# ScalarE's stores issued by GpSimd, the first head's loads put ahead, and the attention outputs split by ScalarE and GpSimd

## The chip, the cores and the metric

The kernel runs on one core of one Trainium2 chip. A core has five engines with an instruction queue each: TensorE (PE, with its weight loads shown apart as PEld), VectorE (DVE), ScalarE (ACT), GpSimd (POOL) and SyncE (SP), and 16 DMA engines that move what any of the queues issues. An engine works through its queue in order: an instruction that waits for a semaphore holds all that stand behind it. The metric is the device time of one execution in microseconds, the median of several.

## The reference

One step of a one-layer decoder over 1024 prompt tokens and 8 x 8 sample tokens: half an FFN, a mixer, and half an FFN again. The mixer joins windowed attention (12 heads of 64) with gated linear attention (4 heads).

```python
h = rmsnorm(x)                        # d_model 1024
x = x + 0.5 * (silu(h @ w1) * (h @ w3)) @ w2            # FFN 1, d_ff 2816
qa, ka, va, qb, kb, vb, rb, glr = split(rmsnorm(x) @ w_in)
qa, ka = rmsnorm(qa) * q_gain, rmsnorm(ka) * k_gain     # per head
oa = merge(dilated_attention(qa, ka, va) + bias)        # windows 128, 512, 2048; prompt
                                      # sample tokens: over 2048 cached keys and the new ones
ob, state = gla(qb, kb, vb, gk)       # chunks of 16
ob = rmsnorm(ob) * silu(rb)
x = x + concat(oa, ob) @ w_out
x = x + 0.5 * (silu(h2 @ w1) * (h2 @ w3)) @ w2          # FFN 2
# returned: x, the keys and values of the windows, the GLA states
```

## The kernel before

Activations lie transposed: 128 channels on the partitions, the 1088 tokens along the free axis. The large products are done in three matmuls each: every operand is split into a high part, rounded to fp32r, and a low part, the rest (`split`, L127: a copy to the high part by one engine, a subtraction for the low part by another; `eh` and `el` choose them, ScalarE and GpSimd where nothing is said). `hH` and `hL` hold the split input of a product, `hl` the split weights, `raw` the weights as loaded.

The program is written as generators, and a scheduler sets each engine's order from its own estimate of times; no order is written out by hand. In time it runs: FFN 1, a norm, the projections, the prompt attention, the output projection, FFN 2.

**The projections** (`inputs`, L309). A unit is 128 columns of the weights in three chunks of tokens, 24 matmuls `psg` each: first those of the linear attention, then values `v`, then queries and keys `q` in turn, then gates `r`. VectorE takes each chunk out of PSUM into a tile `z` (four of them). A chunk of values is turned by TensorE into `psv`, copied to `v` by ScalarE (L431, L433) and stored three ways, to `out_vp`, `vnew` and `out_wv_s` (`turn_values`, L434 to L439). A chunk of queries or keys is normed and stored by GpSimd (`finish_qk`, L473). A chunk of gates is stored to `gsc` by ScalarE (`finish_gate`). Beside this runs the attention of the sample tokens (`sample`, L778): for each of six head pairs SyncE loads a bias `sbias` (L799), keys `kt` (L774) and values `vt` (L794, 512 KB each, six tiles), and ScalarE stores new keys `sko` to `out_wk` and results `soT` to `osc` in two stores (L907). The queries and keys of the sample tokens reach that part through GpSimd's copies `sqk`, `sqs` and into `kt`, which stand behind the stores of L473 in GpSimd's queue.

**The prompt attention** (`attention`, L914) goes over 12 heads. `load(h)` brings queries and keys in as `f` (L929, from `qsc` and `out_kT`, where L473 put them), the bias (L937) and, for each second head, values `va`; VectorE splits them with a cast and a subtraction into `q` and `kk` (L932 to L935); from the second head on GpSimd does the subtraction. Per head: scores `psS` (L962), VectorE adds the bias into `e` (L969), ScalarE's exponential (L982), transposes `psT` and copies `pt`, the weighted sum `psO` (L1022), and VectorE's product into `o` (L1032). When 512 tokens of a head pair are there, `o` is split into `hH` and `hL` (L1035, 12 times). Beside it run the states of the linear attention (`linear_states`, L581; loads `g` from `gsc` and `asc`).

**The output projection** (`out_proj`, `pso`) takes `hH` and `hL`; its weights are split by ScalarE and GpSimd.

A DMA reports its end on a semaphore. In the built program SyncE's and ScalarE's DMAs take turns on eight semaphores (DMAHW0 to 7), GpSimd's on eight others (DMASW0 to 7). A DMA that takes one again first waits, on its own engine's queue, for the end of the transfer that used it last.

Of the kernel before, what the change touches and what calls it, by code (L numbers as in the profile page):

```python
# [9 lines left out]
F32 = mybir.dt.float32  # L10
# [6 lines left out]
P = 128  # L17
# [103 lines left out]
class _Kernel:  # L121
# [299 lines left out]
    def turn_values(self, pool, ps, z, m, ci):  # L421
        nc, a = self.nc, self.a
        cols = slice(128 * m, 128 * m + 128)
        t0, nt = 3 * ci, 3 if ci < 2 else 2
        p = ps.tile([P, 512], F32, tag="b", name="psv")
        for t in range(nt):
            nc.tensor.transpose(p[:, 128 * t : 128 * t + 128], z[:, 128 * t : 128 * t + 128], self.ident)
        if ci == 2:
            nc.tensor.transpose(p[:64, 256:384], z[:, 256:320], self.ident)
        v = pool.tile([P, 3, 128], F32, tag="t1", name="v", bufs=4)  # L430
        nc.scalar.copy(v[:, :nt].rearrange("p t c -> p (t c)"), p[:, : 128 * nt])  # L431
        if ci == 2:
            nc.scalar.copy(v[:64, 2], p[:64, 256:384])  # L433
            nc.scalar.dma_start(out=self.vnew[:, cols], in_=v[:64, 2])  # L434
            nc.scalar.dma_start(
                out=a["wv_s"].rearrange("b (r c) -> b r c", c=768)[:, 2040:2048, cols], in_=v[:64, 2]
            )
            self.vdone = m + 1
        nc.scalar.dma_start(  # L439
            out=a["vp"][128 * t0 : 128 * (t0 + nt), cols].rearrange("(t p) c -> p t c", p=P), in_=v[:, :nt]  # L440
        )

    def finish_gate(self, z, m, ci):
        nc = self.nc
        nc.scalar.activation(z, z, AF.Silu)
        nc.scalar.dma_start(
            out=self.gsc[3 * ci : 3 * ci + 3, :, 5 + m].rearrange("t p r -> p t r"),
            in_=z.rearrange("p (t r) -> p t r", t=3),
        )
# [131 lines left out]
    def linear_states(self, pool, ps):  # L581

        nc, a = self.nc, self.a
        st = pool.tile([P, 9, 64], F32, tag="st", name="st", bufs=2)
        nc.gpsimd.memset(st[:, 0], 0.0)
        ms = pool.tile([P, 3, 36], F32, tag="gms", name="gms")
        qm = []
        for z in range(2):
            t = pool.tile([P, 4, 8, 32], F32, tag="qm", name="qm", bufs=2)
# [46 lines left out]
        for T in range(9):  # L636
            g, kdT, bl = nxt
# [9 lines left out]
            p = ps.tile([P, 512], F32, tag="T", name="psR", bufs=4)  # L647
# [130 lines left out]
    def sample(self, pool, ps, loadk):  # L778
# [18 lines left out]
        for i in range(6):  # L797
# [19 lines left out]
            nc.scalar.dma_start(  # L817
# [88 lines left out]
            for e in range(2):  # L906
                nc.scalar.dma_start(  # L907
                    out=self.osc[i, 64 * e : 64 * e + 64].rearrange("p (b t) -> p b t", t=8), in_=t[:, :, e]
                )
# [4 lines left out]
    def attention(self, inputs, pool, ps):  # L914
        nc = self.nc
        heads = {}

        def load(h):
# [19 lines left out]
            if e == 0:  # L938
                v = pool.tile([P, 8, 128], F32, tag="v", name="va", bufs=2)
                nc.sync.dma_start(  # L940
                    out=v, in_=self.a["vp"][:, 128 * i : 128 * i + 128].rearrange("(t p) c -> p t c", p=P)
                )
            else:
                v = heads[h - 1][3]
            heads[h] = (q, kh, kl, v, b)

        def scores(h, g):

            q, kh, kl, v, b = heads[h]
# [59 lines left out]
        def weigh(h, g, es, pts):  # L1009
            i, e = h // 2, h % 2  # L1010
            r = slice(64 * e, 64 * e + 64)
            v = heads[h][3]
# [20 lines left out]
            if g % 2 and e == 1:  # L1033
                z = slice(512 * (g // 2), 512 * (g // 2) + 512)
                self.split(outs.pop((i, g // 2)), self.hH[:, i, z], self.hL[:, i, z], eh="dve", el="dve")  # L1035
# [5 lines left out]
        load(0)  # L1041
# [105 lines left out]
    def run(self):  # L1147
        nc, tc, a = self.nc, self.tc, self.a
        self.gready, self.done, self.vdone = False, 0, 0
        with ExitStack() as top:  # L1150
# [122 lines left out]
            with ExitStack() as hs:  # L1273
                hpool(hs)
                with ExitStack() as bs:
# [4 lines left out]
                    _interleave(tc, [(self.attention(ip, ap, ps0), 0), (states, 0)])  # L1280
# [166 lines left out]
```

## Time and profile before

| | |
|---|---|
| median of 3 runs | 2401.41 us (2400.91 to 2404.52) |
| the profiled execution | 2401.93 us, span 2400.1 us |
| busy, share of the span | PE 98%, PEld 92%, DVE 48%, ACT 27%, POOL 17% |
| the stages, us from the span's start | FFN 1 48 to 788; norm to 825; projections to 1244; prompt attention to 1519; output projection to 1640; FFN 2 to 2400 |
| PE busy, projections with the sample attention (941 to 1255) | 294.01 of 314 us |
| PE busy, prompt attention (1270 to 1519) | 232.12 of 249 us |
| PE busy, FFN 1 and FFN 2 | 739.70 of 739.70 and 756.76 of 760 us |

The shares are averages over stages with different limits. "Granted clock" is the share of TensorE's full speed that the throttle allowed in a stretch. In the rows a releaser behind an arrow (`<-`) is what ended an engine's idle time; an engine's name with a q (ACTq, SPq) is its queue issuing a DMA.

### The profile page before, as it was taken

To read this page: it belongs to the slowest core of one execution; us is meant where nothing else is said; L and a number is where in the kernel's file an instruction comes from. 1 tells how busy PE (TensorE), PEld (TensorE's weight loads), DVE (VectorE), ACT (ScalarE), POOL (GpSimd) and SP (SyncE) were. 2 spreads that over 40 slices of the span, in tenths; PEclk is the share of its full clock that TensorE was granted. 3 is DMA by queue.
4 is the path that set the end of the run, shared out by engine and by line. 5 is a ranking of instruction groups with operands and counts; after the bars stand their busy time and mean duration, and the time that the engine had idled before them with its cause. 6 is when DMAs were issued, how large, how long until landed. Compare 5 with 4: busy or idle time off the path is not lost.

```text
span 2400.1 us, 38321 instructions
## 1 busy us (share of the span) xinstructions
PE 2341.4 (98%) x16073; PEld 2215.0 (92%) x16073; DVE 1155.9 (48%) x2377; ACT 656.9 (27%) x1347; POOL 408.3 (17%) x303
## 2 busy tenths in 40 slices
PE   7999999999999998999989999999999999999999
PEld 6999999999999987978767767999999999999999
DVE  8452434344342753555538887435444342434333
ACT  5111020101101522545436666334111101020110
POOL 5011020101100400011103231333101101020100
PEclk9999999999999999999999999999999999999999
DMA  7346542524250334599865442414244243111002
GB/s 258 110 162 192 191 152 97 210 97 153 86 196 23 134 131 108 179 342 341 310 184 130 111 115 74 156 36 158 88 163 153 92 154 143 45 53 45 28 17 85
DMA packets 135261, 330.25 MB, mean 138 GB/s; under 512 B 25920, under 2 KB 105264, under 8 KB 127408
## 3 DMA queue, kind: packets, MB, share of 16 engines
q1 hardware_dynamic: 116464, 316.39, 38.7%
q10 hardware_dynamic: 16512, 5.11, 0.9%
q0 software_dynamic: 2112, 6.29, 0.7%
q8 instruction: 126, 2.06, 0.3%
q14 instruction: 47, 0.39, 0.0%
HBM read 300.55 MB, written 134.56 MB: 181 GB/s over the span
## 4 chain that ended last, share of the span: by engine, by line
PE 89%; DVE 5%; DMA 3%; ACT 2%; issue 1%; SPq 1%; POOL 0%; ACTq 0%; DVEq 0%; POOLq 0%
PE ps L306 42%; PE ps L257 21%; PE psg L306 12%; PE pso L306 4%; PE psO L1022 2%; PE psS L962 2%; PE psW L880 1%; PE psT L1001 1%; DMA vt<-in_vin 1%; PE psA L831 1%; DVE hL L155 1%; DVE e L969 1%; PE pss L459 1%; DMA f<-out_kT 0%; DVE rstd L170 0%
## 5 line engine op out<-in xcount | busy, mean ns | idle before, releaser
L306 PE MATMUL ps<-hH,hl 128*128 128x362 f32 (+1 forms) x4224 | 1044.1, 328 | 8.1 <-ACT hl L130 6.8
L306 PEld LDWEIGHTS ps<-hH,hl 128*128 128x128 f32 x4224 | 746.6, 188 | 12.4 <-ACT hl L130 6.7
L306 PE MATMUL ps<-hL,hl 128*128 128x362 f32 (+1 forms) x2112 | 691.5, 328 | 2.9 <-DVE hL L155 2.9
L257 PE MATMUL ps<-g,hl 128*128 128x362 f32 (+1 forms) x3168 | 529.2, 328 | 0.0
L257 PEld LDWEIGHTS ps<-g,hl 128*128 128x128 f32 x3168 | 527.0, 188 | 0.0
L134 POOL TENSOR_TENSOR hl<-raw,hl 128x1024 fp32r<-128x1024 f32 (+1 forms) x98 | 242.8, 2498 | 1223.3 <-ACT hl L130 1223.3
L306 PEld LDWEIGHTS ps<-hL,hl 128*128 128x128 f32 x2112 | 397.5, 188 | 4.9 <-DVE hL L155 3.9
L306 PE MATMUL psg<-hH,hl 128*128 128x384 f32 (+3 forms) x1200 | 312.4, 334 | 0.0
L262 DVE SCALAR_TENSOR_TENSOR xT<-ps,xT 128x362 f32<-128x362 f32 (+1 forms) x384 | 204.6, 534 | 200.3 <-PE ps L257 191.4
L217 ACT ACTIVATE t<-t 128x364 f32<-128x364 f32 x132 | 66.9, 508 | 786.0 <-DVE t L216 785.8
L218 DVE TENSOR_TENSOR t<-ps,rstd 128x364 f32<-128x364 f32 x132 | 70.6, 535 | 417.9 <-PE ps L306 417.9
L306 PEld LDWEIGHTS psg<-hH,hl 128*128 128x128 f32 (+1 forms) x1200 | 211.3, 186 | 12.8 <-issue 8.9
L306 PE MATMUL psg<-hL,hl 128*128 128x384 f32 (+3 forms) x600 | 200.1, 334 | 0.1
L130 ACT CAST hl<-raw 128x1024 fp32r<-128x1024 f32 (+2 forms) x148 | 124.1, 886 | 187.3 <-PE ps L306 109.9
L130 ACT CAST g<-t 128x364 fp32r<-128x364 f32 x132 | 65.2, 494 | 346.8 <-DVE t L219 346.8
L134 DVE TENSOR_TENSOR g<-t,g 128x364 fp32r<-128x364 f32 x132 | 107.1, 813 | 92.8 <-ACT g L130 92.5
L216 DVE TENSOR_TENSOR t<-ps,rstd 128x364 f32<-128x364 f32 x132 | 70.5, 535 | 156.6 <-PE ps L306 155.3
L306 PEld LDWEIGHTS psg<-hL,hl 128*128 128x128 f32 (+1 forms) x600 | 111.7, 186 | 9.3 <-issue 6.7
L134 DVE TENSOR_TENSOR hl<-raw,hl 128x384 fp32r<-128x384 f32 (+3 forms) x178 | 102.9, 587 | 23.9 <-ACT hl L130 19.9
L962 PE MATMUL psS<-kk,q 128*128 128x512 f32 (+2 forms) x288 | 92.2, 411 | 19.6 <-DVE s L969 11.9
L306 PE MATMUL pso<-hH,hl 128*128 128x362 f32 (+1 forms) x384 | 93.6, 325 | 0.2 <-DVE o L1032 0.2
L982 ACT ACTIVATE e<-e,s 128x128 f32<-128x128 f32 (+3 forms) x96 | 74.9, 780 | 43.7 <-DVE s L969 43.1
(205 smaller groups left out, 2007.2 us busy)
## 6 DMA issues: line engine op xcount, KB each, us to landing
out_wk<-in_ck SPq DMA_DIRECT2D x16, 3060.0 KB
out_wv_s<-in_cv SPq DMA_DIRECT2D x16, 3060.0 KB
kt<-in_kin SPq DMA_DIRECT2D x24, 1280.0 KB
vt<-in_vin SPq DMA_DIRECT2D x60, 512.0 KB
raw<-in_w13b SPq DMA_DIRECT2D x22, 1024.0 KB
raw<-in_w13a SPq DMA_DIRECT2D x21, 1024.0 KB
raw<-in_w2a SPq DMA_DIRECT2D x48, 192.0 KB
raw<-in_w2b SPq DMA_DIRECT2D x48, 192.0 KB
```

Of the source, the lines that this page charges most:

```text
L130: nc.scalar.copy(hi, x)
L134: e.tensor_tensor(out=lo, in0=x, in1=hi.bitcast(F32), op=ALU.subtract)
L155: nc.vector.scalar_tensor_tensor(out=self.hL[:, k, s], in0=x, scalar=g, in1=self.hH[:, k, s].bitcast(F32), op0=ALU.mult, op1=ALU.subtract)
L216: nc.vector.tensor_tensor(out=t1[:, :n], in0=p1[:, :n], in1=r, op=ALU.mult)
L217: nc.scalar.activation(t1[:, :n], t1[:, :n], AF.Silu)
L218: nc.vector.tensor_tensor(out=t3[:, :n], in0=p3[:, :n], in1=r, op=ALU.mult)
L257: self.mm(p[:, :n], lhsT=hl[:, wt, j, :], rhs=g[:, gp, :n], start=i == 0, stop=i == 3 * nf - 1)
L262: nc.vector.scalar_tensor_tensor(out=xs, in0=p[:, :n], scalar=0.5, in1=xs, op0=ALU.mult, op1=ALU.add)
L306: self.mm(p[:m, :n], lhsT=hl[:, wt, k, cs], rhs=h[:, k, h0 : h0 + n], start=i == 0, stop=i == 23)
L962: self.mm(p[:, :mm], lhsT=q[:, 128 * n : 128 * n + 128], rhs=kk[:, o : o + mm], start=x == 0, stop=x == 1,)
L982: nc.scalar.activation(e[:, :w], e[:, :w], AF.Exp, scale=-1.0, bias=s[:, j : j + 1], accum_out=s[:, 2:3])
L1022: self.mm(p[64 * n : 64 * n + 64, :128], lhsT=v[:, k, r], rhs=pts[k // 2][k, n], start=k == 0, stop=k == 2 * g + n, tile_position=(0, 64 * n),
```

## The change

Three things are changed. Six `dma_start` calls (54 DMAs in all: 18 to `out_vp`, 6 each to `vnew`, `out_wv_s`, `gsc` and `out_wk`, 12 to `osc`) are issued by GpSimd and no longer by ScalarE. The first head's `load(0)` gets a higher priority in the scheduler, `linear_states` comes first in the interleaving, and the first `va` is loaded there; the `va` tiles move to another pool. The 12 splits of `o` use the default of `split`: the copy by ScalarE, the subtraction by GpSimd.

```diff
@@ turn_values, finish_gate
-            nc.scalar.dma_start(out=self.vnew[:, cols], in_=v[:64, 2])
-            nc.scalar.dma_start(
+            nc.gpsimd.dma_start(out=self.vnew[:, cols], in_=v[:64, 2])
+            nc.gpsimd.dma_start(
                 out=a["wv_s"].rearrange("b (r c) -> b r c", c=768)[:, 2040:2048, cols], in_=v[:64, 2]
             )
             self.vdone = m + 1
-        nc.scalar.dma_start(
+        nc.gpsimd.dma_start(
             out=a["vp"][128 * t0 : 128 * (t0 + nt), cols].rearrange("(t p) c -> p t c", p=P), in_=v[:, :nt]
...
-        nc.scalar.dma_start(
+        nc.gpsimd.dma_start(
             out=self.gsc[3 * ci : 3 * ci + 3, :, 5 + m].rearrange("t p r -> p t r"),
@@ linear_states
         nc.gpsimd.memset(st[:, 0], 0.0)
+        self.load_v(pool, 0)
@@ sample
-            nc.scalar.dma_start(
+            nc.gpsimd.dma_start(
                 out=a["wk"].rearrange("b (r c) -> b r c", c=768)[:, 2040:2048, 128 * i : 128 * i + 128], in_=ko
...
-                nc.scalar.dma_start(
+                nc.gpsimd.dma_start(
                     out=self.osc[i, 64 * e : 64 * e + 64].rearrange("p (b t) -> p b t", t=8), in_=t[:, :, e]
@@ attention
-    def attention(self, inputs, pool, ps):
+    def load_v(self, pool, i):
+        v = pool.tile([P, 8, 128], F32, tag="v", name="va", bufs=2)
+        self.nc.sync.dma_start(
+            out=v, in_=self.a["vp"][:, 128 * i : 128 * i + 128].rearrange("(t p) c -> p t c", p=P)
+        )
+        self.values[i] = v
+
+    def attention(self, inputs, pool, vpool, ps):
...
-            if e == 0:
-                v = pool.tile([P, 8, 128], F32, tag="v", name="va", bufs=2)
...
-            else:
-                v = heads[h - 1][3]
-            heads[h] = (q, kh, kl, v, b)
+            if h % 2 == 0 and h:
+                load_v(i)
+            heads[h] = (q, kh, kl, b)
...
-                self.split(outs.pop((i, g // 2)), self.hH[:, i, z], self.hL[:, i, z], eh="dve", el="dve")
+                self.split(outs.pop((i, g // 2)), self.hH[:, i, z], self.hL[:, i, z])
...
-        load(0)
+        with self.tc.high_priority(offset=300):
+            load(0)
@@ run
-                    _interleave(tc, [(self.attention(ip, ap, ps0), 0), (states, 0)])
+                    _interleave(tc, [(states, 0), (self.attention(ip, ap, gp, ps0), 0)])
```

The scheduler sees the whole program, so the order moves in more places than the diff. Three places follow; numbers behind names are buffer numbers, and "waits" names the semaphores on which a row waits.

ScalarE, in the projections, around the copies of the values (`v_7962` is the last chunk of its unit). Before:

```order
L431 COPY v_7928<-psv_7924 128x384 [waits DMAHW5_49,PE_49]
L439 DMA out_vp<-v_7928 128x3x128 [waits DMAHW1_49,Activation_49]
L431 COPY v_7962<-psv_7958 128x256 [waits DMAHW6_49,PE_49]
L433 COPY v_7962<-psv_7958 64x128
L439 DMA out_vp<-v_7962 128x2x128 [waits DMAHW0_49,Activation_49]
L434 DMA vnew_67<-v_7962 64x128 [waits DMAHW2_49,Activation_49]
L435 DMA out_wv_s<-v_7962 8x8x128 [waits DMAHW4_49]
L431 COPY v_8006<-psv_8002 128x384 [waits PE_49]
L439 DMA out_vp<-v_8006 128x3x128 [waits DMAHW6_49,Activation_49]
```

The same place on ScalarE with the change:

```order
L431 COPY v_7928<-psv_7924 128x384 [waits DMASW5_49,PE_49]
L431 COPY v_7962<-psv_7958 128x256 [waits DMASW6_49,PE_49]
L433 COPY v_7962<-psv_7958 64x128
L431 COPY v_8006<-psv_8002 128x384 [waits DMASW1_49,DMASW0_49,DMASW7_49,PE_49,Activation_49]
L130 CAST hl_8080<-raw_7861 128x512 [waits DMAHW7_49,PE_49]
```

And GpSimd with the change, some way on, where the first stores of the sample results stand among those of L473:

```order
L473 DMA out_kT<-z_8716 128x384 [waits DMASW3_49,DVE_49]
L908 DMA osc_71<-soT_8833 512x1x8 [waits DMASW4_49,Activation_49]
L908 DMA osc_71<-soT_8833 512x1x8 [waits DMASW5_49]
L473 DMA out_kT<-z_8792 128x384 [waits DMASW6_49,DVE_49]
L473 DMA out_kT<-z_8864 128x256 [waits DMASW7_49,DVE_49]
L475 COPY sqk_6871<-z_8864 128x64 [waits Pool_49]
L828 COPY kt_8956<-sqk_6871 128x8x8 [waits DMAHW3_49,PE_49,Pool_49]
```

No store stands between ScalarE's copies any more. On GpSimd the stores of `osc`, which wait for ScalarE's `soT`, now stand between two stores of L473, ahead of the copies for the sample keys.

SyncE, from the last `vt` load on, at the passage from the projections to the prompt attention. Before, and then with the change:

```order
L794 DMA vt_10909<-in_vin 128x1024 [waits PE_49]
L940 DMA va_11135<-out_vp 128x8x128 [waits DMAHW5_49,DVE_49,Pool_49]
L940 DMA va_11349<-out_vp 128x8x128 [waits DMAHW6_49,Activation_49]
L929 DMA f_11121<-qsc_66 64x1024 [waits DMASW2_49,DMAHW0_49,DMASW1_49,DMASW0_49]
L929 DMA f_11121<-qsc_66 64x1024 [waits DMAHW1_49]
L929 DMA f_11127<-out_kT 64x1024 [waits DMASW5_49,DMAHW2_49,DMASW4_49,DMASW3_49]
L929 DMA f_11127<-out_kT 64x1024 [waits DMAHW3_49]
L937 DMA bias_11123<-Z_73 128x1024 [waits DMAHW4_49,PE_49]
L596 DMA g7_11144<-gsc_68 128x640 [waits DMAHW5_49]
```

```order
L795 DMA vt_10909<-in_vin 128x1024 [waits DMAHW7_49,DMAHW0_49,PE_49]
L937 DMA f_11133<-qsc_66 64x1024 [waits DMASW2_49,DMASW3_49,DMASW1_49,DVE_49]
L937 DMA f_11133<-qsc_66 64x1024 [waits DMAHW1_49]
L937 DMA f_11139<-out_kT 64x1024 [waits DMASW6_49,DMAHW2_49,DMASW5_49,DMASW4_49]
L937 DMA f_11139<-out_kT 64x1024 [waits DMAHW3_49]
L945 DMA bias_11135<-Z_73 128x1024 [waits DMAHW4_49,PE_49]
L917 DMA va_11122<-out_vp 128x8x128 [waits DMAHW5_49]
L597 DMA g7_11129<-gsc_68 128x640 [waits DMAHW6_49,Pool_49]
```

The first head's four loads stand right behind the last `vt` and ahead of the values; the DMAHW semaphores on which SyncE waits there no longer alternate with stores of ScalarE.

ScalarE, at the passage from the prompt attention to the output projection. Before, and then with the change:

```order
L1004 COPY pt_14846<-psT_14841 128x512 [waits PE_49,Activation_49]
L1018 COPY rb_14856<-psO_14854 128x128 [waits PE_49]
L130 CAST hl_14891<-raw_14887 128x1024 [waits DMAHW3_49,DMAHW4_49,DMAHW2_49,DMAHW7_49,DMAHW1_49,Pool_49]
L130 CAST hl_14891<-raw_14887 128x1024
L130 CAST hl_14930<-raw_14889 128x1024 [waits DMAHW6_49,DMAHW2_49,Pool_49]
```

```order
L1010 COPY pt_14846<-psT_14841 128x512 [waits PE_49,Activation_49]
L1024 COPY rb_14856<-psO_14854 128x128 [waits PE_49]
L130 CAST hH_11106<-o_14606 128x512 [waits DVE_49]
L130 CAST hl_14891<-raw_14887 128x1024 [waits DMAHW3_49,DMAHW4_49,DMAHW1_49,Pool_49]
L130 CAST hl_14891<-raw_14887 128x1024
```

The copy of the last `o`, which waits for VectorE, now stands ahead of the first weights' copy.

## Rows read from the trace of the kernel before

**Rows 1.** The page: its span, and the chain of work that ended last by engine.

```profile
span 2400.1 us, 38321 instructions
...
PE 89%; DVE 5%; DMA 3%; ACT 2%; issue 1%; SPq 1%; POOL 0%; ACTq 0%; DVEq 0%; POOLq 0%
```

**Rows 2.** Busy time in stretches of the span: from and to, length, then of each engine the busy time with its instructions in brackets, the granted TensorE clock, the DMA engines' busy share and GB/s.

```profile
941.00:1255.00 314.00, 294.01 (x2273) 245.71 (x2272) 150.50 (x311) 135.72 (x286) 31.99 (x84) 0.97 0.79 267
...
1244.00:1276.00 32.00, 19.76 (x164) 14.11 (x164) 22.52 (x59) 14.81 (x38) 10.82 (x9) 0.79 0.71 186
...
1270.00:1400.00 130.00, 121.45 (x1502) 94.69 (x1500) 110.20 (x331) 86.88 (x238) 36.87 (x26) 0.97 0.43 116
```

**Rows 3.** For what TensorE waited in the whole span: total us, times, longest.

```profile
PE psS L962 <- DVE s L969: 11.9, 11, 2.0
PE psv L427 <- ACT v L431: 8.8, 1, 8.8
PE psS L962 <- DVE kk L934: 6.9, 1, 6.9
...
PE psO L1022 <- ACT rb L1018: 4.7, 4, 2.2
```

**Rows 4.** ScalarE and its queue in order of time, around 949: start, us, instruction, and the idle time before it with what ended it.

```profile
937.04 0.26 ACT L433 COPY v<-psv 64x128 f32<-64x128 f32 x1
954.63 0.38 ACTq L439 DMA_DIRECT2D out_vp<-v  x1
...
956.82 0.64 ACTq L435 DMA_DIRECT2D out_wv_s<-v  x1
957.51 0.48 ACT L431 COPY v<-psv 128x384 f32<-128x384 f32 x1 [20.20 <-DMA vt<-in_vin]
```

**Rows 5.** The chain of waits through the same stretch: start, us, what.

```profile
936.74 4.19 PE psg L306 x24
...
946.20 10.60 DMA vt<-in_vin
```

**Rows 6.** Busy time in stretches, columns as in rows 2.

```profile
958.00:962.00 4.00, 3.96 (x14) 3.93 (x15) 1.42 (x3) 1.56 (x4) 0.00 (x0) 0.50 1.01 374
...
1000.00:1200.00 200.00, 196.76 (x1630) 157.50 (x1623) 113.03 (x238) 98.35 (x210) 24.90 (x66) 1.00 0.93 328
1200.00:1244.00 44.00, 43.90 (x329) 37.26 (x327) 9.82 (x21) 12.21 (x25) 1.42 (x5) 1.00 0.49 160
```

**Rows 7.** For what SyncE's queue waited from 960 to 1240: total us, times, longest.

```profile
SPq L794 <- PE psW L880: 73.9, 25, 11.2
```

**Rows 8.** A store on GpSimd's queue in order of time.

```profile
1045.82 0.54 POOL L473 DMA_DIRECT2D out_kT<-z  x1 [10.88 <-DVE z L468]
```

**Rows 9.** A store of the sample results on ScalarE's queue in order of time.

```profile
1044.99 0.55 ACTq L907 DMA_DIRECT2D osc<-soT  x1
```

**Rows 10.** DMA issues from 941 to 1244: how many, KB each, median us from issue to landing.

```profile
qsc<-z POOLq DMA_DIRECT2D x12, 192.0 KB, 6.0
```

**Rows 11.** SyncE's queue in order of time, at the start of the prompt attention.

```profile
1238.26 6.00 SPq L929 DMA_DIRECT2D f<-qsc  x2
1245.28 1.11 SPq L929 DMA_DIRECT2D f<-out_kT  x2
...
1253.65 1.10 SPq L929 DMA_DIRECT2D f<-qsc  x2
```

**Rows 12.** VectorE in order of time, in the same stretch.

```profile
1244.28 0.21 DVE L404 TENSOR_TENSOR zr<-psg,rstd 128x64 f32<-128x64 f32 x1
1247.33 1.03 DVE L932 CAST q<-f 128x1024 fp32r<-128x1024 f32 x1 [2.83 <-DMA f<-qsc]
1248.39 1.22 DVE L933 TENSOR_TENSOR q<-f,q 64x1024 fp32r<-64x1024 f32 x1
1249.98 0.69 DVE L934 CAST kk<-f 128x1024 fp32r<-128x1024 f32 x1 [0.36 <-DMA f<-out_kT]
```

**Rows 13.** The chain of waits in the same stretch.

```profile
1247.54 5.51 DMA g<-asc
...
1255.99 7.79 DMA f<-out_kT
```

**Rows 14.** What writes `hH` from 1270 to 1519, different shapes apart: times, shortest/median/longest ns, first and last start.

```profile
L132 DVE CAST hH<-o x11: 421/428/2131, 1296.2 to 1511.4; 128x512 fp32r<-128x512 f32 x11
L134 DVE TENSOR_TENSOR hL<-o,hH x11: 673/689/2327, 1298.0 to 1512.6; 128x512 fp32r<-128x512 f32 x11
...
L130 ACT CAST hH<-so x1: 512/512/512, 1325.0 to 1325.0; 128x384 fp32r<-128x384 f32 x1
...
L134 POOL TENSOR_TENSOR hL<-gob,hH x9: 456/730/1169, 1342.6 to 1508.2; 128x256 fp32r<-128x256 f32 x8, 128x128 fp32r<-128x128 f32 x1
```

**Rows 15.** The chain of waits from 1270 to 1519.2, shares by line.

```profile
by line: PE psO L1022 17.6%; PE psS L962 17.1%; PE psT L1001 10.8%; issue 6.2%; DVE e L969 5.8%; PE psE L709 3.3%; DVE hL L134 2.9%; PE psD L666 2.8%; ACT e L982 2.5%; DVE o L1032 2.4%; PE psE L704 2.4%; DVE hH L132 2.2%; DVE kk L934 2.2%; 
```

**Rows 16.** All engines in order of time, at the start of the output projection.

```profile
1516.21 3.92 ACT L130 CAST hl<-raw 128x1024 fp32r<-128x1024 f32 x4
...
1516.40 1.97 PE L1022 MATMUL psO<-pt,va 128*64 128x128 f32 x30 [0.89 <-ACT rb L1018]
...
1518.30 0.43 PE L306 MATMUL pso<-hH,hl 128*128 128x364 f32 x1
...
1518.47 0.59 DVE L1032 TENSOR_TENSOR o<-psO,rb 64x128 f32<-64x128 f32 x2 [2.48 <-PE psO L1022]
```

More of the change, by code (lines that the diff above doesn't have):

```diff
@@ L937, in load, with load_v @@
             nc.sync.dma_start(out=b, in_=bass.AP(z.tensor, z.offset + 127, [[GW - 1, P], [1, NP]]))
-            if e == 0:
-                v = pool.tile([P, 8, 128], F32, tag="v", name="va", bufs=2)
-                nc.sync.dma_start(
-                    out=v, in_=self.a["vp"][:, 128 * i : 128 * i + 128].rearrange("(t p) c -> p t c", p=P)
-                )
-            else:
-                v = heads[h - 1][3]
-            heads[h] = (q, kh, kl, v, b)
+            if h % 2 == 0 and h:
+                load_v(i)
+            heads[h] = (q, kh, kl, b)
+        def load_v(i):
+            self.load_v(vpool, i)
         def scores(h, g):
-            q, kh, kl, v, b = heads[h]
+            q, kh, kl, b = heads[h]
             out = []
@@ L1011, in weigh @@
             r = slice(64 * e, 64 * e + 64)
-            v = heads[h][3]
+            v = self.values[i]
             if g % 2 == 0 and e == 0:
@@ L1149, in run @@
         self.gready, self.done, self.vdone = False, 0, 0
+        self.values = {}
         with ExitStack() as top:
```

## The prediction

> **What bounds it now.** I read the page first: TensorE's own work is 89% of the chain that ended last, of 2400.1 us [rows 1]. The FFNs, two thirds of the time, are not touched, so the change can only win back idle time of TensorE, or time at the lower clock, between 941 and 1520 us. The view by stretches shows how much there is: 20 us idle in 941 to 1255, 12 of 32 us at the start of the prompt attention, 8.5 of 130 us further on in it [rows 2]. Then the table of waits, which puts names to it: 8.8 us once for ScalarE's copy `v`, 6.9 us once for the first keys' cast on VectorE, and in the prompt attention 11.9 us in eleven waits for VectorE's `s` and 4.7 us for ScalarE's `rb` [rows 3]. The change has one part for each of the first three.
>
> **A, the stores on GpSimd.** ScalarE ended its copy at 937.30 and its next store could be issued only at 954.63; the following copy, for which TensorE stood from 949 on, began at 957.51 after 20.20 us, 17 of them before that first store [rows 4]. The data of the stores had long been there. The chain reaches the last of these stores through the landing of a `vt` load, 10.60 us [rows 5]: a load of SyncE that shares nothing with the store but the semaphore. In the order of before each store stands between two copies and waits on a DMAHW semaphore; with the change no store is there, and GpSimd's stores wait only on DMASW, for older stores of GpSimd. So the 8.8 us go. After the gap TensorE ran four microseconds at a granted 0.50, which is 1.2 of 2.4 GHz [rows 6]; at full clock the same work takes 2.0. A = 10.8 us. Lower bound 7, if the clock stays low and a wait is left as long as the longest for `s`, 2.0 [rows 3]; upper 11.
>
> Can TensorE keep the lead? From 1000 to 1200 the DMA engines are 0.93 busy and TensorE idles 3.2 of 200 us [rows 6]. But SyncE's queue waited there 73.9 us for TensorE to free `vt` tiles [rows 7]: loads follow TensorE, not the other way, and the share falls to 0.49 at the end of the stretch [rows 6]. The whole stretch moves forward together.
>
> What the stores cost GpSimd: 54 issues at 0.54 us, the time of one of its stores now [rows 8], against 0.55 on ScalarE [rows 9], are 29 us on an engine busy 32 of 314 us [rows 2]. Beside TensorE that is nothing. The stores of `osc` have 512 pieces each, of a kind that GpSimd does not issue before; below, the same 0.54; above, the 6.0 us that its stores take to land [rows 10], if it were held for so long. I take 0.54, since both engines' issue times are alike.
>
> The Trainium skill ("DMA: Bandwidth & Descriptors", section "Issuing engines are not separate DMA queues") says that all queues feed the same 16 DMA engines and that issuing from another engine saves only the issuing time. By that A would be nothing and the sum 2392. The gap in rows 4 is not issuing time but a wait ahead of it, which the page does not speak of.
>
> **B, the first head's loads.** Now SyncE's `f` loads of head 0 stand behind both `va`; their issue takes from 1238.26 to 1246.39, because the semaphores alternate with stores, and head 1's follow at 1253.65 [rows 11]. VectorE, done with the gates at 1244.49, waits 2.83 us for queries and ends the keys' cast at 1250.67 [rows 12]. With the change all four loads stand right behind the last `vt`, so that they can land before the projections end. VectorE's order still puts the casts behind the gates: 1244.5 + 1.03 + 1.22 + 0.69 (the durations in rows 12) gives 1247.5, which is 3.2 us earlier. The path goes on through head 1's loads, in the chain with 5.51 us for `g` and 7.79 us for `f` [rows 13]. These need head 0's first `f` tile, which the subtraction frees at 1249.61 [rows 12]; the 4 us from there to 1253.65 are the semaphores. So 3.2 for the tile and 4 for them: 7 us earlier. I take 7, since the chain runs through head 1; bounds 3 (head 0's gain alone) and 10 (with clock won back, 0.79 there [rows 2]).
>
> **C, the splits.** Eleven casts of 428 ns and eleven subtractions of 689 ns (medians, the longest 2131 and 2327 [rows 14]) leave VectorE in the stretch. On the chain they are 2.2% and 2.9% of 249.2 us [rows 15], 12.7 us. ScalarE gets 12 copies; the nearest, 128x384, took 512 ns [rows 14], so 0.6 each, 7 us in all: it has room (86.88 of 130 busy [rows 2]) but TensorE waits for it too, 4.7 us for `rb` [rows 3]. GpSimd gets 12 subtractions at twice the 730 ns of 128x256 [rows 14], less what an instruction costs anyway: an estimate of 1.3 each, 15 us, with 36.87 of 130 busy [rows 2]. VectorE is only one of several engines that end last here, so I take half of the 12.7: C = 6, from nothing to 12.
>
> The Trainium skill ("SBUF — State Buffer", section "Who interferes with whom") says that a VectorE instruction with two SBUF inputs and a GpSimd instruction that reads SBUF exclude each other for a whole instruction. By that 12 subtractions of 1.3 us would block VectorE up to 15 us, against the 12.3 us of work at median length (eleven times 0.428 + 0.689) that leave it: C would be nothing, and the sum 2387. The trace agrees that some such thing is there: medians of 428 and 689 ns stand beside longest ones of 2131 and 2327 [rows 14].
>
> **E, a loss.** At the passage to the output projection ScalarE now begins the weights' copy at 1516.21, four of them in 3.92 us, and `pso` starts at 1518.30, as the last `psO` ends at 1518.37 [rows 16]. With the change the last `o`'s copy stands ahead of it in ScalarE's order; that `o` is done 0.7 us after the last `psO` (1519.06 [rows 16]). So 0.7 + 0.6 for the copy + 1.0 for the first weights' copy: `pso` starts 2.4 us after `psO`, and some low clock after it, an estimate of 1 from rows 6. E = 3.5, from 2 to 4.5. The first product's low weights come later still on GpSimd, behind the last subtraction; I count that as covered by the matmuls on high weights.
>
> **Sum.** 2400.1 - 10.8 - 7 - 6 + 3.5 = 2379.8 us of span; the profiled execution took 1.8 us more than its span, so 2381.6, and it lay 0.5 above the median: **2381 us**. With all lower bounds (7, 3, 0, -4.5) 2396, with all upper ones (11, 10, 12, -2) 2370.
>
> **Rivals.**
> 1. *A is given back.* The transfers run on the same 16 engines, 0.93 busy from 1000 on, and TensorE waits for `vt` or `kt` instead: 2381 + 10.8 = 2392. For it: that share. Against it: SyncE's waits for TensorE.
> 2. *C is nothing:* ScalarE takes VectorE's place in the waits of `psO` and `psT`, or GpSimd's subtractions stretch VectorE's work: 2387.
> 3. *The loads are early, but it does not help:* casts remain behind the gates in VectorE's order and head 1 comes no earlier: B is 3, 2385.
> 4. *Slower: GpSimd's queue.* In it the stores of `osc` now stand, waiting for `soT`, ahead of stores of normed queries and keys. If `soT` comes late, the four `z` tiles stay occupied, VectorE cannot take the next chunk and TensorE stops. The store behind it waited 10.88 us for its own data, and was issued at 1045.82, 0.8 us after `osc` on ScalarE [rows 8, 9]: today the two are about even. Three free tiles are three chunks of 24 matmuls, 4.19 us each [rows 5], so 12 us of slack. From 12 us on each microsecond counts, six times: with 17 us it is 6 x 5 = 30, 2411. The same end comes if a store holds GpSimd near the 6.0 us of its landing.
>
> **How the numbers follow.** Forecast 0.55; rival 1 0.13; rival 2 0.13; rival 3 0.05; the first two together (2398) 0.05; rival 4 0.09. The range 2370 to 2397 is the sum's two ends; it holds rivals 1 to 3 and most of the forecast, and leaves out some 0.17. A difference of 0.2%, 4.8 us, is about what a measurement of this kernel can tell. Faster by more: the forecast, 0.11 of rival 1, all of rivals 2 and 3: 0.84. The same: 1 and 2 together and what is left of rival 1 and 4, 0.09. Slower: 0.07.
>
> **What would show it.** A: no wait of `psv` for ScalarE over 1 us, and the clock whole from 949 to 962. B: `psS` waits 3 to 4 us, not 6.9, and TensorE's idle time in the 32 us from the end of the projections falls from 12 to about 5. C: `hH<-o` and `hL<-o` on ScalarE and GpSimd, waits of `psS` for `s` shorter. E: a wait of the first `pso` for ScalarE of 2 to 3 us. I am wrong if TensorE idles more than 6 us between 1000 and 1244 (old clock), if GpSimd's new stores take over 1 us each, or if `rb` and `e` take over the waits of `s`.

## The result, and the profile after

The changed kernel takes 2384.25 us (median of 4 runs, 2383.22 to 2385.45), the kernel before 2401.16 (2397.02 to 2404.52) on the same chip: a ratio of 0.9931, with a 95% interval of 0.9913 to 0.9948. It is 0.7% faster, 17 us, where 20 were forecast. The profiled execution has a span of 2383.0 us. Its page, span and chain, as [rows 1]:

```profile
span 2383.0 us, 38378 instructions
...
PE 91%; DVE 4%; DMA 2%; issue 1%; ACT 1%; POOL 0%; SPq 0%; DVEq 0%; ACTq 0%; POOLq 0%
```

The chain has two points more of TensorE, and less of VectorE, DMA and ScalarE. For what TensorE waited, as [rows 3] (line numbers up to 8 higher than before, since the file grew):

```profile
PE psS L968 <- DVE s L975: 6.1, 11, 1.3
...
PE psS L968 <- DVE kk L942: 3.2, 1, 3.2
PE psW L881 <- DMA vt<-in_vin: 2.8, 3, 1.7
PE pso L306 <- ACT hl L130: 2.4, 1, 2.4
...
PE psO L1028 <- ACT rb L1024: 0.4, 1, 0.4
```

The 8.8 us of `psv` are not there at all; the keys' cast costs 3.2 us and not 6.9, the waits for `s` 6.1 and not 11.9, `rb` 0.4 and not 4.7. New are 2.4 us in which the first `pso` waits for ScalarE, and `psW` waits for `vt` loads, 2.8 us.

To see where the time went, I read six moments from both timelines (us from the span's start, in the profiled executions):

| | before | after | earlier by | won in this stretch |
|---|---|---|---|---|
| the 720th `psg`, just behind the gap at 949 | 968.50 | 955.61 | 12.9 | 12.9 |
| end of the last `psg` | 1243.90 | 1236.45 | 7.4 | -5.5 |
| first `psS` | 1250.82 | 1239.68 | 11.1 | 3.7 |
| end of the last `psO` | 1518.36 | 1497.16 | 21.2 | 10.1 |
| first `pso` | 1518.30 | 1499.52 | 18.8 | -2.4 |
| end of the span | 2400.1 | 2383.0 | 17.1 | -1.7 |

Of the first 12.9 us, 2.1 were there by 870, ahead of the change's places: from 858 to 864 the mean granted clock was 0.72 in the execution before and 1.00 in the one after, and among the kernels below it is 0.72 in some (e1, e3 and e7 among them) and 1.00 in others (e2, e5 and e9 among them). No edit touches this place, and I don't count the 2.1 as the change's; but where one kernel was profiled twice (after and e5, e4 and e6) both have 1.00, so whether it is chance or the order of the work stays open. The gap itself gave 10.8: from the 600th `psg`, ahead of it, to the 720th it is 32.04 us before and 21.25 after.

**A.** GpSimd's queue in the stretch of [rows 4], start, us, instruction, idle time and what ended it:

```profile
944.52 0.75 POOL L439 DMA_DIRECT2D out_vp<-v  x1 [3.75 <-ACT v L431]
948.24 0.72 POOL L439 DMA_DIRECT2D out_vp<-v  x1 [2.96 <-ACT v L433]
948.95 0.56 POOL L434 DMA_DIRECT2D vnew<-v  x1
949.51 0.62 POOL L435 DMA_DIRECT2D out_wv_s<-v  x1
```

The three stores that held ScalarE for 17 us are issued as soon as ScalarE's copy is there. And the price of four kinds of store, the first a kind that GpSimd issued before, from 930 to 1240 us (busy us, mean ns, idle before):

```profile
L473 POOL DMA_DIRECT2D qsc<-z x18 | 9.9, 552 | 75.9 <-DVE z L468 75.8
L439 POOL DMA_DIRECT2D out_vp<-v x11 | 8.2, 748 | 30.5 <-ACT v L431 17.5 <-ACT v L433 12.9
L908 POOL DMA_DIRECT2D osc<-soT x12 | 8.2, 694 | 40.2 <-ACT soT L906 40.2
L446 POOL DMA_DIRECT2D gsc<-zr x6 | 4.6, 762 | 17.3 <-ACT zr L445 17.3
```

A store of `osc` with its 512 pieces costs 694 ns to issue, one of `gsc` 762, against 0.54 us that I took. Nothing is near the 6.0 us of the upper bound. But between 1000 and 1236 some of the lead is lost again. Two stretches there (columns as in [rows 2]):

```profile
1000.00:1018.00 18.00, 16.33 (x134) 13.48 (x134) 9.97 (x19) 10.53 (x23) 2.60 (x8) 1.00 0.98 298
1018.00:1022.00 4.00, 4.00 (x35) 2.14 (x38) 0.00 (x0) 0.00 (x0) 0.00 (x0) 0.57 0.98 392
```

In the first TensorE stood 1.67 us, `psW` waiting for a `vt` load; behind it the granted clock fell to half, 0.57 in the mean of these four microseconds. That is not all of the 5.5 us: idle time grew by 1.4 (3.24 to 4.65) and the half clock cost 1.7, so some 2.3 are left, and they are busy time of TensorE at full clock. The same 2158 matmuls behind the 720th `psg` keep it busy 272.0 to 272.7 us in before, e2, e3 and e8, and 274.9 to 275.7 in e1, e4 to e7 and e12, the kernels with all 54 stores moved, with the clock whole in all of them. What makes them longer, the runs don't show.

**B.** SyncE's queue and VectorE at the start of the attention, as [rows 11, 12]:

```profile
1219.25 1.16 SPq L937 DMA_DIRECT2D f<-qsc  x2
1220.57 1.90 SPq L937 DMA_DIRECT2D f<-out_kT  x2
...
1238.93 1.11 SPq L937 DMA_DIRECT2D f<-qsc  x2
```

```profile
1236.83 0.21 DVE L404 TENSOR_TENSOR zr<-psg,rstd 128x64 f32<-128x64 f32 x1
1236.96 0.68 DVE L940 CAST q<-f 128x1024 fp32r<-128x1024 f32 x1
...
1238.93 0.69 DVE L942 CAST kk<-f 128x1024 fp32r<-128x1024 f32 x1
```

The first head's loads are issued 17 us ahead of the last `psg`, so VectorE goes from the gates straight to the casts, and head 1's queries are loaded 2.5 us after the last `psg` (1238.93 against 1236.45), where it was 9.8 us before (1253.65 against 1243.90). In the 32 us from the last `psg` on, TensorE idles 7.0 us, not 12 (the prediction had 5).

**C.** What writes `hH` and `hL` of `o`, as [rows 14], and the whole attention before and after, from the first `psS` to the last `psO` (columns as in [rows 2]):

```profile
L130 ACT CAST hH<-o x12: 603/619/644, 1279.5 to 1497.9; 128x512 fp32r<-128x512 f32 x12
L134 POOL TENSOR_TENSOR hL<-o,hH x12: 1270/1284/1463, 1283.5 to 1498.6; 128x512 fp32r<-128x512 f32 x12
```

```profile
1250.80:1518.40 267.60, 247.64 (x2902) 193.24 (x2902) 212.45 (x646) 177.16 (x475) 69.89 (x49) 0.95 0.40 109
```

```profile
1239.70:1497.20 257.50, 241.58 (x2901) 187.61 (x2901) 199.14 (x624) 180.09 (x483) 84.72 (x62) 0.97 0.41 115
```

The prices were right: 0.62 us on ScalarE, 1.28 on GpSimd. The last two rows tell more. It is the same work, some 2900 matmuls in both; yet TensorE is busy 247.64 us in the one and 241.58 in the other, at a mean granted clock of 0.95 and 0.97. Of the 10.1 us won, 6.1 are busy time, matmuls that ran faster, and 4.0 are idle time (19.96 to 15.92 us).

**E.** The start of the output projection, as [rows 16], and the clock right after it:

```profile
1499.37 2.94 ACT L130 CAST hl<-raw 128x1024 fp32r<-128x1024 f32 x3
1499.52 0.67 PE L306 MATMUL pso<-hH,hl 128*128 128x364 f32 x1 [2.35 <-ACT hl L130]
```

```profile
1499.50:1503.00 3.50, 3.48 (x12) 3.49 (x13) 0.00 (x0) 2.81 (x3) 3.50 (x3) 0.54 0.57 157
```

`pso` waits 2.35 us for the first weights' copy, and runs its first 3.5 us at 0.54.

### The profile page after: what moved, and what is told of

It reads as the page before. It is cut to its first block, busy times and chain, and to the rows that moved or that the text cites. A ratio compares the mean times of both kernels' runs of the same rounds, so it can differ in the third digit from the quotient of the medians.

```text
span 2383.0 us, 38378 instructions
## 1 busy us (share of the span) xinstructions
PE 2337.3 (98%) x16073; PEld 2209.9 (93%) x16073; DVE 1135.6 (48%) x2353; ACT 661.9 (28%) x1359; POOL 459.0 (19%) x369
## 4 chain that ended last, share of the span: by engine, by line
PE 91%; DVE 4%; DMA 2%; issue 1%; ACT 1%; POOL 0%; SPq 0%; DVEq 0%; ACTq 0%; POOLq 0%
PE ps L306 43%; PE ps L257 21%; PE psg L306 12%; PE pso L306 4%; PE psO L1028 2%; PE psS L968 2%; PE psT L1007 1%; PE psA L832 1%; DMA vt<-in_vin 1%; PE psW L881 1%; DVE hL L155 1%; DVE rstd L170 1%; PE pss L459 1%; DVE e L975 0%; PE psD L667 0%
## 5 line engine op out<-in xcount | busy, mean ns | idle before, releaser
L306 PEld LDWEIGHTS psg<-hH,hl 128*128 128x128 f32 (+1 forms) x1200 | 209.0, 184 | 13.8 <-issue 10.1
L306 PEld LDWEIGHTS psg<-hL,hl 128*128 128x128 f32 (+1 forms) x600 | 110.6, 184 | 10.9 <-issue 8.3
L219 DVE TENSOR_TENSOR t<-t,t 128x364 f32<-128x364 f32 x132 | 74.4, 565 | 18.3 <-ACT t L217 4.7
```

The source lines that it names most:

```text
L219: nc.vector.tensor_tensor(out=t3[:, :n], in0=t3[:, :n], in1=t1[:, :n], op=ALU.mult)
L306: self.mm(p[:m, :n], lhsT=hl[:, wt, k, cs], rhs=h[:, k, h0 : h0 + n], start=i == 0, stop=i == 23)
```

## The experiments

All were timed in five rounds against the kernel before, those of e1 to e4, e5 to e8 and e9 to e12 on one chip each. The differences are against 2399.6, 2399.4 and 2399.0 us.

### One part alone: e1, e2, e3

e1 is the kernel before with the six `nc.scalar.dma_start` written `nc.gpsimd.dma_start`. e2 is the change without that and without the splits. e3 is one line:

```diff
-                self.split(outs.pop((i, g // 2)), self.hH[:, i, z], self.hL[:, i, z], eh="dve", el="dve")
+                self.split(outs.pop((i, g // 2)), self.hH[:, i, z], self.hL[:, i, z])
```

Expected of e1:

> Only the 54 stores go from ScalarE to GpSimd. Theory (the stores held ScalarE's copies through semaphores shared with SyncE's loads): no wait of psv for ScalarE, the clock whole from 949 to 962, 10.8 us won by the middle of the values, some 4 us of it given back to later vt loads: 2394, 0.3% faster than before. Rival (the same 16 DMA engines, nothing won): 2401 with the 8.8 us in another wait before 1244.

Expected of e2:

> Only the first head's loads are put ahead (with the order of the two generators and the va tiles), stores on ScalarE, splits on VectorE. Theory of my sum: psS waits 3.2 us for the first keys' cast and not 6.9, and head 1 follows earlier: 2394. Rival (the early place helps only with the stores gone, since SyncE's loads still alternate on the semaphores with ScalarE's stores): the loads land late as before, 2399 to 2401.

Expected of e3:

> Only the 12 splits of o go to ScalarE and GpSimd. Theory: 6 us won between 1270 and 1519, 4 us lost at the start of the output projection (pso waits 2.4 us for the weights' copy, then 3.4 us at half clock): 2399, which is the same as before. Rival (ScalarE and GpSimd become what TensorE waits for): nothing won and 4 us lost, 2405.

(The profiled execution of before, 2401.93 us, lies 2 us above the median of the 24 runs beside these three, so differences of single profiles are good to some 3 us.) e1 took 2393.31 us, ratio 0.9975 (0.9964 to 0.9985), as expected. No wait of `psv` for ScalarE is in its table; the last `psg` ended at 1234.41, 9.5 us earlier than before. But the 4 us that I had later `vt` loads take back are not there: `psW` waits for one once, 0.3 us, and 1.8 us of the lead go. Head 1's queries come 4.8 us after the last `psg` in e1 (1239.20), against 9.8 before, with the loads not yet put ahead. e2 took 2400.07, ratio 1.0000 (0.9992 to 1.0009): nothing, the time of my rival. e3 took 2391.73, ratio 0.9972 (0.9963 to 0.9980): 8 us won, where I expected none, and without the loss at `pso`. The scheduler, with other estimates, put the first weights' copies ahead of the last `o` there: in its trace `pso` starts at 1510.34, the last `psO` ends at 1510.41.

In e2 the first keys were in time: `psS` began 3.9 us after the last `psg`, as forecast for the change, so of my rival "the loads land late as before" does not hold. But the rest of the start did not follow. SyncE's queue in e2, and then for what it waited from 1215 to 1262:

```profile
1233.23 6.25 SPq L937 DMA_DIRECT2D f<-out_kT  x2
...
1243.99 0.33 SPq L597 DMA_DIRECT2D g<-gsc  x1
1249.17 0.38 SPq L599 DMA_DIRECT2D g<-asc  x1
...
1250.19 2.02 SPq L937 DMA_DIRECT2D f<-qsc  x2
```

```profile
SPq L937 <- DMA gsc<-zr: 5.3, 1, 5.3
SPq L599 <- DMA gsc<-zr: 4.8, 1, 4.8
...
SPq L945 <- DMA osc<-soT: 3.0, 1, 3.0
```

Two issues of `f` take 6.25 us, between `g<-gsc` and `g<-asc` 5.2 us pass, and head 1's queries come at 1250.19, 7.4 us after the last `psg` (1242.79), against 2.5 in the change. SyncE stands in turn behind ScalarE's stores: the loads of keys, of `asc` and of the bias that wait here read nothing of `gsc` or `osc`. (Before, loads of `f` and of the bias wait 4.2 and 4.6 us for stores to `gsc`; in the change, e7 and e11 SyncE waits for no such store in this stretch.) What the early load wins, TensorE then waits for again, 4.55 us at 1259.44, for ScalarE's `rb`. That copy stood behind an exponential of the linear attention, which waited for a load of `g`:

```profile
1258.82 0.31 ACT L616 ACTIVATE gw<-g 128x128 f32<-128x128 f32 x1 [4.50 <-DMA g<-gsc]
```

### Two parts of three: e5 to e8, and the last split

e5 is the change once more. e6 is the kernel of e4, which is the change but for this:

```diff
-                self.split(outs.pop((i, g // 2)), self.hH[:, i, z], self.hL[:, i, z])
+                k = dict(eh="dve", el="dve") if i == 5 and g == 3 else {}
+                self.split(outs.pop((i, g // 2)), self.hH[:, i, z], self.hL[:, i, z], **k)
```

e7 is the change with the 12 splits on VectorE, e8 the change with the 54 stores on ScalarE.

Expected of e4:

> The whole change, but the very last of the 12 splits stays on VectorE, so that nothing stands ahead of the first weights' copy on ScalarE. Theory: the wait of the first pso for ScalarE (2.4 us) and the half clock behind it (1.7 us lost) go: 2380, 4 us faster than the change. Rival (the weights' copy is late for another reason, or GpSimd's low weights become what pso waits for): 2384, the wait stays under another name.

Expected of e5:

> The whole change, unaltered, beside the next three on the same chip. Expected 2384, as before; the difference of two executions shows how far the vt waits (2.8 us) and the clock between 1000 and 1240 vary: if they are of the change itself, 4 us and more of the first part are given back again.

Expected of e6:

> The kernel of e4 once more, on the same chip as e5. Theory (2.4 us of waiting and 1.7 us of half clock at the first pso): 3.5 to 4.5 us faster than e5. Rival (the difference of e4 was one of executions): within 1.5 us of e5.

Expected of e7:

> The change without the splits: stores on GpSimd and the first head's loads ahead, the 12 splits on VectorE. Theory (the parts add up): 6 us for the stores and 3 to 7 for the loads, 2388 to 2391, with nothing won between the first psS and the end of psO except by head 1. Rival (the loads are worth nothing in time, as alone in e2): 2393, as e1.

Expected of e8:

> The change without the stores, which stay on ScalarE: loads ahead and splits on ScalarE and GpSimd. Theory (parts add up): psv waits its 8.8 us again, the splits win 7 to 8, 2390 to 2392. Rival (the loads win only where VectorE is relieved too): less than 2389, with more won between the first psS and the end of psO than the 7.3 us of e3.

| | us | ratio to before, interval | last `psg` ends | first `psS` to last `psO` | of these TensorE busy, idle |
|---|---|---|---|---|---|
| before | | | 1243.90 | 267.6 | 247.6, 20.0 |
| e4 last split back | 2380.73 | 0.9930, 0.9917 to 0.9942 | 1233.53 | 256.8 | 241.3, 15.5 |
| e5 the change | 2383.52 | 0.9936, 0.9924 to 0.9949 | 1234.21 | 257.7 | 242.9, 14.8 |
| e6 last split back | 2380.62 | 0.9924, 0.9911 to 0.9936 | 1236.02 | 258.1 | 241.2, 17.0 |
| e7 no splits (stores and loads) | 2384.20 | 0.9940, 0.9927 to 0.9952 | 1235.77 | 262.7 | 241.3, 21.4 |
| e8 no stores (loads and splits) | 2392.24 | 0.9968, 0.9956 to 0.9980 | 1244.29 | 257.9 | 243.1, 14.8 |
| e1 stores alone | 2393.31 | 0.9975, 0.9964 to 0.9985 | 1234.41 | 267.6 | 246.5, 21.0 |
| e2 loads alone | 2400.07 | 1.0000, 0.9992 to 1.0009 | 1242.79 | 267.5 | 245.1, 22.4 |
| e3 splits alone | 2391.73 | 0.9972, 0.9963 to 0.9980 | 1243.28 | 260.3 | 243.4, 17.0 |

(The last three columns are one profiled execution each.) e4 and e5 came out as expected (2380 and 2384). Four things follow. First, the parts do not add up. Alone, stores win 6 us and loads nothing; together, in e7, 15. That is more than either theory allowed for (2388 to 2391, or 2393). Without the stores the loads add nothing to the splits either: e8 wins 7 us, e3 alone 8, and in e8 `psv` waits its 8.8 us again, as expected. Second, e7 is as fast as the change within the measurement: in the change the splits win 5 us in the attention (262.7 to 257.7) and lose most of it at `pso`. With the last split back on VectorE (e6) 2.9 us of it return, less than the 3.5 to 4.5 expected, on the same chip as e5 (five runs each, 2379.84 to 2382.84 and 2382.03 to 2385.95); in e6's table of waits the only wait of `pso` is 0.2 us for `o`, in e5's it is

```profile
PE pso L306 <- ACT hl L130: 2.3, 1, 2.3
```

Third, with all stores on GpSimd the last `psg` ends between 1233.5 and 1236.5 in one profile each; e4 and e6, one kernel, lie 2.5 us apart. So part of what is given back between 1000 and 1240 varies from one execution to the next, and 7.4 us in the first profile after was the low end. Fourth, the splits take idle time away, and about what I had taken: 3.0 us from before to e3, 7.6 from e2 to e8, 6.6 from e7 to e5. What else the attention wins is busy time: e7 against e1 (loads, given the stores) has 0.4 us more idle and 5.2 less busy, at a mean granted clock of 0.97 and 0.95.

### Why ScalarE's queue held the copies: e9

```diff
-        nc.scalar.copy(v[:, :nt].rearrange("p t c -> p (t c)"), p[:, : 128 * nt])
+        nc.vector.tensor_copy(v[:, :nt].rearrange("p t c -> p (t c)"), p[:, : 128 * nt])
...
-            nc.scalar.copy(v[:64, 2], p[:64, 256:384])
+            nc.vector.tensor_copy(v[:64, 2], p[:64, 256:384])
```

Expected of e9:

> The kernel before, with all stores on ScalarE, but the value copies (L431, L433) on VectorE. Theory (the copies were late only because they stood behind the stores): the stores are still issued near 954, but psv waits under 1 us and the half clock at 952 to 962 is gone; by the end of the projections 7 to 10 us won, 2393 as in e1. Rival (the copy or psv itself was slow, or the DMA engines): the wait of 8.8 us stays, for VectorE now.

It took 2397.10 us, ratio 0.9992 (0.9983 to 1.0001), not the 2393 that I expected. The first half came as the theory said. ScalarE's queue:

```profile
949.70 12.41 ACTq L439 DMA_DIRECT2D out_vp<-v  x2
962.98 0.48 ACTq L434 DMA_DIRECT2D vnew<-v  x1
```

The stores still stand, two of them from 949.70 for 12.41 us, and TensorE no longer minds: from 950 to 962 it is busy 12.00 of 12 us at a clock of 1.00, and the 720th `psg` comes 13.2 us earlier than before (2.45 of them were there at the 600th, ahead of the gap). But behind the same stores stands the next thing that TensorE needs from ScalarE, the split squares of the queries, and from 935 to 1241 it waited for

```profile
PE pss L459 <- ACT sqhl L130: 5.8, 2, 4.8
```

with a half clock behind that, 0.62 in 966 to 975. The wait moved by one stage: it is ScalarE's queue that was held, whatever stood in it. By the last `psg` 3.0 us were left, 0.5 without those 2.45.

### Which stores hold the start of the attention: e10, e11

Both are e7, with part of the stores back on ScalarE: in e10 those of `gsc`, `out_wk` and `osc` (24), in e11 those of `out_vp`, `vnew` and `out_wv_s` (30).

Expected of e10:

> e7 with only the 30 value stores on GpSimd; gates, sample keys and sample results (24 stores) stay on ScalarE; loads ahead, splits on VectorE. Theory (the loads at the start of the attention are held by the semaphores that SyncE shares with the stores of gates and sample results): psv does not wait, but head 1's queries are issued 7 us after the last psg as in e2 (2.5 in e7), 2391 to 2394. Rival (the value stores are all that matters): 2384 as e7.

Expected of e11:

> The counterpart: the 24 stores of gates, sample keys and sample results on GpSimd, the 30 value stores on ScalarE; loads ahead, splits on VectorE. Theory: psv waits its 8.8 us with the half clock behind it, head 1's queries are issued 2 to 3 us after the last psg, 2391 to 2394. Rival (the start of the attention is won by something else): head 1's queries late, 2398 to 2400.

e10 took 2393.80 us, ratio 0.9977 (0.9968 to 0.9987), e11 2393.37, 0.9975 (0.9966 to 0.9985). `psv` does not wait in e10, and SyncE issued head 1's queries late in e10 and early in e11, as expected:

```profile
1227.89 4.72 SPq L937 DMA_DIRECT2D f<-out_kT  x2
...
1242.54 1.10 SPq L937 DMA_DIRECT2D f<-qsc  x2
```

```profile
1225.74 1.12 SPq L937 DMA_DIRECT2D f<-out_kT  x2
...
1244.64 1.10 SPq L937 DMA_DIRECT2D f<-qsc  x2
```

That is 6.0 us after the last `psg` in e10 (1236.59) and 2.5 in e11 (1242.16); in e11 `psv` waits its 8.7 us. So the value stores make the gap at 949, and the late ones the slow start. In time both are needed: with either part of the stores back the change without splits loses 8 to 9 us (0.9977 and 0.9975 against 0.9940 for e7, intervals apart). Where in the trace the late stores' share lies is less clear: from the first `psS` to the last `psO` e10 took 264.7 us with late loads and e11 266.4 with early ones, where e7 took 262.7; and e10's profile is of its fastest execution, 2388.69 us, 5 below its median. In all of these the order of the attention differs by what the scheduler made of it, and what e7 wins over e1 there is clock and not idle time; whether head 1's load or the order brings it stays open.

### Does GpSimd's half of the splits pay: e12

```diff
-                k = dict(eh="dve", el="dve") if i == 5 and g == 3 else {}
+                k = dict(eh="dve" if i == 5 and g == 3 else "act", el="dve")
```

Expected of e12:

> e6 with only the high copies (11 of 12) on ScalarE; all 12 subtractions on VectorE. Theory (what wins is the time taken from VectorE, 25 us in all, of which the subtractions are 15): half and more of the 3.6 us that the splits won between e7 and e6 is lost, 2382 to 2383. Rival (GpSimd's subtractions cost VectorE as much as they save, as two engines that exclude each other): 2380 or less.

It took 2377.76 us (2375.65 to 2379.80), ratio 0.9911 (0.9898 to 0.9925), the fastest of all: the time of the rival. The attention in e6 and in e12:

```profile
1239.20:1497.40 258.20, 241.17 (x2902) 186.92 (x2902) 198.92 (x624) 182.32 (x486) 86.10 (x63) 0.98 0.40 114
```

```profile
1238.80:1495.70 256.90, 241.40 (x2902) 188.66 (x2902) 200.34 (x635) 182.60 (x486) 73.55 (x52) 0.97 0.41 115
```

Eleven more subtractions are done by VectorE, and its busy time goes from 198.92 to 200.34 us only. Some of VectorE's groups in both, e6 and then e12 (busy us, mean ns):

```profile
L622 DVE TENSOR_TENSOR qm<-gw,hmask 128x256 f32<-128x256 f32 x18 | 11.6, 682 | 0.3
...
L612 DVE TENSOR_TENSOR gw<-g 128x128 f32<-128x128 f32 x9 | 9.2, 1021 | 3.4 <-DMA g<-gsc 3.3
...
L134 DVE TENSOR_TENSOR hL<-o,hH 128x512 fp32r<-128x512 f32 x1 | 2.8, 2775 | 0.0
```

```profile
L134 DVE TENSOR_TENSOR hL<-o,hH 128x512 fp32r<-128x512 f32 x12 | 10.9, 910 | 0.5 <-ACT hH L130 0.5
L622 DVE TENSOR_TENSOR qm<-gw,hmask 128x256 f32<-128x256 f32 x18 | 9.9, 583 | 0.4
...
L612 DVE TENSOR_TENSOR gw<-g 128x128 f32<-128x128 f32 x9 | 6.9, 772 | 4.4 <-DMA g<-gsc 4.4
```

The subtractions go from 2.8 to 10.9 us, 8.1 more, and two groups of two-input products from 20.8 to 16.8 us, 4.0 less. That looks as if GpSimd's subtractions had cost VectorE much of what they took from it, as the rival says. The trace of e6 does not bear it out. GpSimd does hold VectorE up there, but with other work (GpSimd's queue, then VectorE's):

```profile
1341.67 2.59 POOL L941 TENSOR_TENSOR q<-f,q 64x1024 fp32r<-64x1024 f32 x1 [2.98 <-PE psS L968]
1344.34 2.50 POOL L943 TENSOR_TENSOR kk<-f,kk 128x1024 fp32r<-128x1024 f32 x1
```

```profile
1341.96 2.45 DVE L612 TENSOR_TENSOR gw<-g 128x128 f32<-128x128 f32 x1
...
1345.15 2.57 DVE L622 TENSOR_TENSOR qm<-gw,hmask 128x256 f32<-128x256 f32 x2
```

`gw<-g` starts 0.3 us behind GpSimd's subtraction for the queries and ends 0.2 us behind it, after 2.45 us; the three of its kind beside which GpSimd does nothing take 0.29. In e6 fifteen of VectorE's `gw`, `qm` and `kk` took at least a quarter longer than undisturbed ones. Eleven of them ran beside GpSimd's subtractions for queries and keys, three beside `kdT` and one beside that of `so`, work that GpSimd does before too; only one also touches one of the eleven subtractions of `o`, with its end. Counted over `gw`, `qm`, `kk`, `hL` and `hH`, this extra time is 18.0 us in e6, 13.5 in e12, and 22.8 in e7, where none of the splits is on GpSimd (21.4 before). So it goes by what the order puts side by side, and a price of the moved subtractions on VectorE is not shown. The Trainium skill ("SBUF — State Buffer", section "Who interferes with whom") states that a VectorE instruction with two SBUF inputs contends with a GpSimd instruction that reads SBUF; the 2.45 us of `gw` against 0.29 agree with it. In time, no run shows that the subtractions win anything by leaving VectorE. e6 and e12 ran on different chips, and their intervals overlap: e12 is not seen to be slower, as the theory had it, and that it is 3 us faster is not shown.

## Why the prediction was right, and where it was not

The time fell within the range, and near the forecast (2384 against 2381). The sum came nearer than its terms: A brought 5.5 us less by the last `psg` than at the gap, 2.1 us that are not counted as the change's made up part of it, and B and C were booked to parts that do not win them alone. Step by step:

- **A, the gap.** Right: `psv` does not wait, 10.8 us at the gap, forecast 10.8. That stores waiting for SyncE's loads held ScalarE's queue is borne out by e9, where the copies are gone from it, two stores still stand for 12.41 us and the next work behind them is late, and by e2, where SyncE's own queue is held at the other end by stores whose data it does not need. The trace names a `vt` load as what released the third of the stores at the gap [rows 5]; for the first, which came 17 us late, it names nothing, and no run changes the semaphores alone.
- **"The whole stretch moves forward together."** This step failed. Between 968 and the last `psg`, 5.5 us were given back in the profile of after, 1.8 to 4.3 in the others with all stores moved. In the profile after, 3.1 us of it are idle time and half clock, and what shows there is a `vt` load that comes late (1.67 us at 1016); the rest is longer busy time at full clock, which all these kernels have. Rival 1 was half right, and I had argued against it with SyncE's waits for TensorE, 73.9 us in total; a total says nothing of the one load that comes late. Counted from the 600th `psg`, A was 5.4 us at the last `psg` after and 6.5 to 9.0 in the others with all stores moved, not 10.8; alone, in e1, it came to 6 us of time.
- **B.** The first keys: 3.2 us of wait as worked out, 3.7 won against 3.2. Head 1's queries 7.3 us earlier relative to the last `psg` (2.5 against 9.8), forecast 7. But it was wrong to book this to the loads: four of the seven were the semaphores, which A takes away. e1, the stores without the loads, has head 1's queries 4.8 us after the last `psg`, so 5.0 of the 7.3 are there already; e2, the loads without the stores, has them after 7.4 and wins nothing in time. TensorE's idle time in the 32 us behind the last `psg` fell to 7.0, not to 5.
- **C.** From the first `psS` to the last `psO` 10.1 us, where the sum had 9.8 (6 for the splits and 3.8 for the rest of B). The prices on ScalarE and GpSimd were right, and so was 6 for the splits (3.0 to 7.6 us of idle time in three pairs). Two things were not: GpSimd's half of them wins nothing that shows (e12), and what I had put down as waits for head 1 shows as busy time at a better clock. Rival 2 falls: `rb` went from 4.7 to 0.4 us, and the stretched work of VectorE lies beside GpSimd's older subtractions (e12's section).
- **E.** Right: 2.35 us of wait, and 1.7 lost behind it, at half clock; 2.4 and 1 in the sum (its terms 0.7, 0.6 and 1.0 add up to 2.3). e6 wins 2.9 back by keeping the last split on VectorE, and e8 shows the same wait of 2.4 us. In e3 the scheduler's order spares it: the loss hangs on the order alone.
- **Rivals 3 and 4.** GpSimd's queue was never late: a store costs 0.55 to 0.78 us, and no `psg` is in TensorE's table of waits. Rival 3 is what happens without the stores (e2), not in the change.

The fastest version measured is e12: the change, with the subtractions on VectorE and the last split there whole, 2377.8 us, 0.9% faster than before.

## What to carry to other kernels

A store on a compute engine's queue is not free because its issue takes half a microsecond: look what semaphore it waits on and who else takes turns on it; here a store came 17 us late in a queue whose stores wait in turn with another queue's loads, and with it came every copy behind it. Parts that touch the same wait don't add up, so cost them together, and check with two-of-three runs. And before work is moved to the end of a busy engine's queue, see what stands behind it at the next passage: the last of twelve splits lost most of the 5 us that the splits won in the attention.

## What the runs showed of the hardware

The clock is a term of its own. Among these kernels the same 2900 matmuls of the attention kept TensorE busy from 240.1 us (e10) to 247.6 us (before), and not simply by how long it idled: e10 idled 24.6 us there, before 20.0. Most of the difference is granted clock. By an estimate, with the busy time at the lower level counted by the clock granted in it, all fourteen profiles come to 233.5 to 236.2 us; what the lower level took is 13.5 us before, 6.2 after, 6.7 in e10 and 5.0 in e6. What decides it these runs don't show; a few us of a difference between two kernels can be this alone.

VectorE's products of two SBUF tiles were held up beside GpSimd's subtractions, `gw<-g` from 0.29 us to 2.45. Its work on scores from PSUM was not: `e<-psS,bias` of 128x512 takes 0.69 us in e6, beside GpSimd's work and without it.
